# Attention value products reordered around two transposes, one MLP transpose moved, and stationary weight tiles shifted by 128 bytes

## The chip, the cores and the metric

The kernel runs on one core of a Trainium2 chip. The metric is device time in microseconds (us). The engines are named as in the profile: PE is TensorE (PEld its weight loads), ACT is ScalarE, DVE is VectorE, POOL is GpSimd, SP is SyncE, which issues most of the DMA transfers.

## The reference

One differential-attention layer and one MoBA block layer over 256 tokens of width 1024, each followed by a squared-ReLU MLP, all in float32:

```
def layer_step(h, layer):
    mix = diff_attention(h, ...) if layer == 0 else moba_attention(h, ...)
    h = layer_norm(ALPHA * h + mix, ln1_g[layer], ln1_b[layer])
    mlp = square(relu(h @ w_up[layer])) @ w_down[layer]
    return layer_norm(ALPHA * h + mlp, ln2_g[layer], ln2_b[layer])

# diff_attention, per head of 128 value columns (8 heads, two score maps each):
a = softmax(s1) - lam * softmax(s2)          # causal, with a relative-position bias
o = a @ v
o = o * rsqrt(mean(o * o) + eps) * subln_g * (1 - lam_init)
mix = o.reshape(256, 1024) @ w_out
```

The 256 tokens form two blocks of 128 queries, called halves here (h = 0 and 1).

## The kernel before

**Weights.** The weights arrive as 96 units of 128 x 2048, 48 for each layer, and each unit in two pieces of 1024 columns. SP fetches a piece into one of five `raw` tiles. `head()` has ACT round it to the high part `whi`; `piece()` has DVE form the low part `wlo` = raw - whi and then issues the fetch five pieces on. The parts live in seven `whi` and seven `wlo` tiles that are reused in turn. `bg(n)` puts up to n such pieces between other work; when it is not forced it goes by a credit that matmuls earn.

**Products.** Every operand of a product is split in high and low parts, and `three()` issues three matmuls for each product: high by high, and the two mixed ones. It has two forms. In the row form (lines 141 to 143) an activation block is the stationary operand and 512 (at the very end 256) columns of the weights stream past it. In the stationary form (lines 145 to 147) a 128 x 128 block of the weights is the stationary operand and 256 token columns of the activations stream past it. The trace names the moving operand first, then the stationary one: `whi,act_hi` at line 141, `act_hi,whi` at line 145. The stationary form makes a part of the projections ahead of both attentions and the MLP's up products of column groups 2 to 7; the row form makes the rest, among it the values, the output projection (`mix`), the up products of groups 0 and 1 (`up_rows`) and the down products.

**The end of the first attention.** Pairs 0 to 7 are the heads. For each, `turn(p)` transposes the softmaxed scores on PE (line 515) into a bank of the two `ps_c`, `turned(p)` has ACT copy that bank to `aT` (line 524), and `values(p)` multiplies by V (lines 539 to 541) into two of the four `ps_a` banks: one 128-column matmul for the first half of the queries and two for the second. The heads' output O is collected four heads at a time: `rms` squares it on ACT (line 575, eight squares), makes the reciprocal root on DVE or POOL, `scale(h)` multiplies a half (line 581). `o_turn(p0, h)` then transposes a half of four heads on PE (line 292, four matmuls into a `ps_c` bank), and ACT and DVE split it into `act_hi` (line 72) and `act_lo` (line 76), which `mix` uses as stationary operand. `mix(h, c, G0)` sums over heads 0 to 3, `mix(h, c, G1)` over heads 4 to 7.

**The MLP.** The column groups 0 and 1 are made in row form: `up_rows(c, h, g)` gives half h of group c, `g` is the half of the inner sum. `square` on ACT makes the squared ReLU, and `up_turn(c, h)` transposes it on PE (line 776, four matmuls). From group 2 on, `up(c, j)` uses the stationary form.

Engines run their instructions in program order, which is the order of the code; nothing else sorts them. The SBUF places follow from the tile pools. Every `whi` and `wlo` tile starts 192 bytes past a multiple of 256; the activations' tiles (`act_hi`, `act_lo`, `h_hi`, `h_lo`) start 128 bytes past one. These places were read from the built kernels, not from the trace.

Of the kernel before, what the change touches and what calls it, by code (L numbers as in the profile page):

```python
# [21 lines left out]
F32R = mybir.dt.float32r  # L22
# [30 lines left out]
def trunk(ctx: ExitStack, tc: tile.TileContext, x, first, units, lam_a, subln, rel_bias,  # L53
# [7 lines left out]
    dram = ctx.enter_context(tc.tile_pool(name="dram", bufs=1, space=bass.MemoryType.DRAM))  # L61


    small.tile([P, 24], F32, name="pad", bufs=1)

    def bank(tag):
        return psum.tile([P, 512], F32, name="ps_" + tag, tag=tag,
                         bufs={"a": 4, "b": 2, "c": 2}[tag])
# [16 lines left out]
    def fetch(q):  # L85

        if q < NU * PER:
            v, s = divmod(q, PER)
            raws[q] = wpool.tile([P, PIECE], F32, name="raw", bufs=RAWS)
            nc.sync.dma_start(raws[q], units[v, s])  # L90

    def head():

        v, s = divmod(state["head"], PER)
        if v >= NU:
            return False
        if s == 0 and v not in split:
            if v >= AHEAD and v - AHEAD not in free:
                return False
            split[v] = (wpool.tile([P, 2048], F32R, name="whi", bufs=AHEAD),  # L100
                        wpool.tile([P, 2048], F32R, name="wlo", bufs=AHEAD))
        c = slice(s * PIECE, (s + 1) * PIECE)
        nc.scalar.activation(split[v][0][:, c], raws[state["head"]], AF.Copy)  # L103
        state["head"] += 1
        return True
# [15 lines left out]
    def bg(most=8, force=False):  # L121

        while most > 0 and (force or state["credit"] >= 1.0 / PER):
            if not piece():
                state["credit"] = min(state["credit"], 1.0)
                return
            state["credit"] -= 1.0 / PER
            most -= 1
# [209 lines left out]
    def attention(layer, u0):  # L338
# [4 lines left out]
        with tc.tile_pool(name=f"attn{layer}", bufs=2) as pool, \  # L343
# [19 lines left out]
            def v_first(u):  # L363

                if u == 0:
                    for h in range(2):
                        pv[0, h] = bank("a")
                split[u] = (wpool.tile([P, 2048], F32R, name="whi", bufs=AHEAD),
                            wpool.tile([P, 2048], F32R, name="wlo", bufs=AHEAD))
                hi, lo = (w.rearrange("p (k c) -> p k c", k=4) for w in split[u])  # L370
                for k in range(4):
                    kk = 4 * u + k
                    split_to(act[0][:, kk], act[1][:, kk], chunks[kk][:, :S])
                    split_to(hi[:, k], lo[:, k], chunks[kk][:, S:])
                    if 2 <= kk < NK - 1:
                        fetch(kk + 2)
                    if kk == 6:
                        nc.scalar.dma_start(scr, line)
                    a = [at(kk, h) for h in range(2)]
                    for h in range(2):  # L380
                        nc.tensor.matmul(pv[0, h], a[h][0], hi[:, k], start=kk == 0, stop=False)  # L381
                    for h in range(2):
                        nc.tensor.matmul(pv[0, h], a[h][1], hi[:, k], start=False, stop=False)
                    for h in range(2):
                        nc.tensor.matmul(pv[0, h], a[h][0], lo[:, k], start=False, stop=kk == NK - 1)
                state["piece"] = state["head"] = (u + 1) * PER
                state["credit"] += PACE
                used.add(u)
# [139 lines left out]
                        nc.vector.tensor_copy(dst, src[:, :, ::-1])  # L528
                AT[p] = a

            def values(p):

                a = AT.pop(p)
                if diff:
                    if p % 4 == 0:
                        po[0], po[1] = bank("a"), bank("a")
                    c = slice(p * P, (p + 1) * P)
                    o = slice((p % 4) * P, (p % 4 + 1) * P)
                    nc.tensor.matmul(po[0][:, o], a[:, 0, 0:128], V[:, 0, c], start=True, stop=True)
                    nc.tensor.matmul(po[1][:, o], a[:, 0, 128:256], V[:, 0, c], start=True, stop=False)  # L540
                    nc.tensor.matmul(po[1][:, o], a[:, 0, 256:384], V[:, 1, c], start=False, stop=True)
                    return
                if p % 2 == 0:
                    po[p] = bank("a")
                o = po[p - p % 2][:, (p % 2) * S:(p % 2 + 1) * S]

                r = [slice(m * 64, (m + 1) * 64) for m in range(2)]
                v = [slice((2 * p + m) * 64, (2 * p + m + 1) * 64) for m in range(2)]
                for m in range(2):
                    nc.tensor.matmul(o[r[m]], V[:, 0, v[m]], a[:, m, 0:256], start=True, stop=False)  # L550
                for m in range(2):
                    nc.tensor.matmul(o[r[m], 128:], V[:, 1, v[m]], a[:, m, 256:384], start=False, stop=True)
# [33 lines left out]
            def o_turn(p0, h):  # L586
                transposed(O[p0][:, h], p0, h, gsub, True)
# [53 lines left out]
            if diff:  # L641
                turn(5)
                v_unit(u0 + 10, 1, 0)
                halves_hi(7)
                softmax_a(6)
                halves_lo(7)
                turned(5)
                scale = rms(0, [O[0][:, h] for h in range(2)], nc.gpsimd)
                bg(1)
                softmax_b(6)  # L650
                scores(7)
                turn(6)
                v_unit(u0 + 11, 1, 1)
                turned(6)
                softmax_a(7)
                bg(1, True)
                softmax_b(7)
                for h in range(2):
                    v_out(1, h)
                for h in range(2):  # L660
                    scale(h)
                bg(1, True)
                turn(7)
                turned(7)
                o_turn(0, 0)
                o_turn(0, 1)
                bg(2, True)
                for p in range(4, 8):
                    values(p)
                mix(0, 0, G0)  # L670
                scale = rms(4, po, nc.vector)
                scale(0)
                scale(1)
                bg(3, True)
                mix(0, 1, G0)
                mix(1, 0, G0[:2])
                o_turn(4, 0)
                mix(1, 0, G0[2:])
                o_turn(4, 1)
                bg(2, True)  # L680
                for c in range(2):
                    mix(0, c, G1)
                    if c == 0:
                        bg(1, True)
                    ln_add(0, c * 512, c * 512 + 512, pw[0, c])
                ln_apply(layer, 0, 512)
                bg(1, True)
                mix(1, 1, G0)
            else:
                turn(5)  # L690
                mix(0, 0, G0[:2])
                values(4)
                turned(5)
                mix(0, 0, G0[2:])
                halves_hi(7)
                softmax_a(6)
                halves_lo(7)
                softmax_b(6)
                scores(7)
                values(5)  # L700
                turn(6)
                mix(0, 1, G0)
                softmax_a(7)
                turned(6)
                collect(4)
                bg(1, True)
                softmax_b(7)
                bg(1, True)
                values(6)
                mix(1, 0, G0)  # L710
                turn(7)
                turned(7)
                bg(2, True)
                mix(0, 0, G1[:2])
                values(7)
                collect(6)
                mix(0, 1, G1[:2])
                bg(1, True)
                for c in range(2):
                    mix(0, c, G1[2:])  # L720
                    ln_add(0, c * 512, c * 512 + 512, pw[0, c])
                ln_apply(layer, 0, 512)
                mix(1, 1, G0)
# [16 lines left out]
    def mlp(layer, u0, then):  # L740
# [3 lines left out]
        with tc.tile_pool(name=f"mlp{layer}", bufs=2) as pool:  # L744
# [13 lines left out]
            def up_rows(c, h, g, then=None):  # L758
                if g == 0:
                    SQ[c, h] = bank("b")  # L760
                hi, lo = unit(u0 + 2 * c + g, k=4)
                for k in range(4):
                    three(SQ[c, h], (hi[:, k], lo[:, k]), at(4 * g + k, h), True, 1 / 8,
                          g == 0 and k == 0, g == 1 and k == 3)
                    if then and k % 2 == 0:
                        then(k // 2)
                if h == 1:
                    used.add(u0 + 2 * c + g)
# [67 lines left out]
            up_turn(1, 0)  # L836
            bg(2)
            up_rows(1, 1, 0)
            bg(2)
            up_rows(1, 1, 1)  # L840
            SQ[1, 1] = square(SQ[1, 1])
            up_turn(0, 1)
            bg(2)
            up(2, 0)
            bg()
# [135 lines left out]
```

## Time and profile before

| what | value |
|---|---|
| median of 3 runs | 592.87 us (592.8 to 593.11) |
| the profiled execution's own time | 593.63 us |
| its span | 591.6 us |
| PE busy | 580.2 us, 98% |
| PEld / DVE / ACT / POOL busy | 87% / 64% / 54% / 2% |
| granted TensorE clock | 0.995 of full speed (1.00 in the stretches looked at) |

The span runs from the first to the last recorded instruction; the execution's own time has 2.03 us more around it. A prediction made in the span's microseconds is carried over to the median by the difference of 0.76 us between this execution's own time and the median.

### The profile page before, as it was taken

To read this page: it belongs to the slowest core of one execution; us is meant where nothing else is said; L and a number is where in the kernel's file an instruction comes from. 1 tells how busy PE (TensorE), PEld (TensorE's weight loads), DVE (VectorE), ACT (ScalarE), POOL (GpSimd) and SP (SyncE) were. 2 spreads that over 40 slices of the span, in tenths; PEclk is the share of its full clock that TensorE was granted. 3 is DMA by queue.
4 is the path that set the end of the run, shared out by engine and by line. 5 is a ranking of instruction groups with operands and counts; after the bars stand their busy time and mean duration, and the time that the engine had idled before them with its cause. 6 is when DMAs were issued, how large, how long until landed. Compare 5 with 4: busy or idle time off the path is not lost.

```text
span 591.6 us, 9649 instructions
## 1 busy us (share of the span) xinstructions
PE 580.2 (98%) x3768; PEld 515.6 (87%) x3768; DVE 378.5 (64%) x692; ACT 318.3 (54%) x540; POOL 13.1 (2%) x45
## 2 busy tenths in 40 slices
PE   9999999999999999999999999999999999999993
PEld 7999978889899899898889999878899899899883
DVE  5798778976744644543978677697785544554236
ACT  6676787257654655552447555642785564554100
POOL 2000020000000000000000000000000000000000
PEclk9999999999999999999999999999999999999998
DMA  8996736447745836755259744151798556553002
GB/s 300 327 337 229 243 116 212 174 150 268 271 172 207 277 126 237 248 168 191 83 170 344 256 150 155 54 178 36 242 324 288 175 183 214 187 170 107 1 0 71
DMA packets 35548, 113.03 MB, mean 191 GB/s; under 512 B 3872, under 2 KB 8880, under 8 KB 35504
## 3 DMA queue, kind: packets, MB, share of 16 engines
q1 hardware_dynamic: 34144, 107.95, 53.8%
q0 software_dynamic: 1152, 4.19, 2.4%
q8 instruction: 29, 0.48, 0.3%
q10 hardware_dynamic: 208, 0.29, 0.1%
q14 instruction: 15, 0.12, 0.1%
HBM read 111.35 MB, written 1.07 MB: 190 GB/s over the span
## 4 chain that ended last, share of the span: by engine, by line
PE 97%; DMA 1%; DVE 1%; ACT 0%; SPq 0%; issue 0%; DVEq 0%
PE ps_a L143 13%; PE ps_a L142 13%; PE ps_b L145 13%; PE ps_a L141 13%; PE ps_b L147 12%; PE ps_b L146 12%; PE ps_b L141 4%; PE ps_b L143 4%; PE ps_b L142 4%; PE ps_a L462 2%; PE ps_c L515 1%; PE ps_c L292 1%; DMA raw<-in_first 1%; PE ps_a L550 1%; PE ps_c L776 1%; PE ps_a L381 1%
## 5 line engine op out<-in xcount | busy, mean ns | idle before, releaser
L115 DVE TENSOR_TENSOR wlo<-raw,whi 128x1024 fp32r<-128x1024 f32 x188 | 222.8, 1220 | 55.1 <-ACT whi L103 54.7
L103 ACT ACTIVATE whi<-raw 128x1024 fp32r<-128x1024 f32 x188 | 190.1, 1052 | 71.6 <-PE ps_a L143 52.5
L145 PE MATMUL ps_b<-act_hi,whi 128*128 128x256 f32 x640 | 179.8, 281 | 0.0
L146 PE MATMUL ps_b<-act_lo,whi 128*128 128x256 f32 x640 | 177.5, 277 | 0.0
L147 PE MATMUL ps_b<-act_hi,wlo 128*128 128x256 f32 x640 | 177.5, 277 | 0.0
L145 PEld LDWEIGHTS ps_b<-act_hi,whi 128*128 128x128 f32 x640 | 120.2, 188 | 1.5 <-issue 0.7
L146 PEld LDWEIGHTS ps_b<-act_lo,whi 128*128 128x128 f32 x640 | 120.7, 189 | 0.5
L147 PEld LDWEIGHTS ps_b<-act_hi,wlo 128*128 128x128 f32 x640 | 120.3, 188 | 0.0
L143 PE MATMUL ps_a<-whi,h_lo 128*128 128x512 f32 x248 | 97.7, 394 | 0.0
L142 PE MATMUL ps_a<-wlo,h_hi 128*128 128x512 f32 x248 | 97.2, 392 | 0.0
L141 PE MATMUL ps_a<-whi,h_hi 128*128 128x512 f32 x248 | 96.5, 389 | 0.0
L74 DVE TENSOR_TENSOR h_lo<-sqr,h_hi 128x512 fp32r<-128x512 f32 x24 | 16.6, 693 | 77.7 <-ACT h_hi L72 77.7
L142 PEld LDWEIGHTS ps_a<-wlo,h_hi 128*128 128x128 f32 x248 | 46.6, 188 | 10.3
L141 PEld LDWEIGHTS ps_a<-whi,h_hi 128*128 128x128 f32 x248 | 46.6, 188 | 9.9
L143 PEld LDWEIGHTS ps_a<-whi,h_lo 128*128 128x128 f32 x248 | 46.6, 188 | 9.3
L753 ACT ACTIVATE relu<-ps_b 128x512 f32<-128x512 f32 x32 | 19.1, 596 | 65.9 <-PE ps_b L147 55.0
L482 ACT ACTIVATE t<-t,mx 128x256 f32<-128x256 f32 x64 | 28.4, 445 | 31.5 <-DVE mx L479 31.5
L141 PE MATMUL ps_b<-whi,act_hi 128*128 128x512 f32 x96 | 39.1, 407 | 0.0
L143 PE MATMUL ps_b<-whi,act_lo 128*128 128x512 f32 x96 | 37.7, 393 | 0.0
L142 PE MATMUL ps_b<-wlo,act_hi 128*128 128x512 f32 x96 | 37.6, 391 | 0.0
L141 PE MATMUL ps_a<-whi,act_hi 128*128 128x512 f32 x80 | 32.3, 403 | 0.0
L142 PE MATMUL ps_a<-wlo,act_hi 128*128 128x512 f32 x80 | 31.5, 393 | 0.0
(140 smaller groups left out, 587.3 us busy)
## 6 DMA issues: line engine op xcount, KB each, us to landing
raw<-in_units SPq DMA_DIRECT2D x188, 512.0 KB, 4.6
bias<-scr SPq DMA_DIRECT2D x16, 256.0 KB, 5.3
lnp<-in_ln_g POOLq DMA_DIRECT2D x4, 512.0 KB, 4.5
lnp<-in_ln_b POOLq DMA_DIRECT2D x4, 512.0 KB, 5.4
raw<-in_first SPq DMA_DIRECT2D x5, 384.0 KB, 6.6
xres<-in_x SPq DMA_DIRECT2D x1, 1024.0 KB, 5.9
out<-xres SPq DMA_DIRECT2D x2, 256.0 KB, 2.1
out<-xres SPq DMA_DIRECT2D x4, 128.0 KB, 1.9
```

The source lines that it names most:

```text
L74: nc.vector.tensor_tensor(lo, src, hi.bitcast(F32), op=ALU.subtract)
L103: nc.scalar.activation(split[v][0][:, c], raws[state["head"]], AF.Copy)
L115: nc.vector.tensor_tensor(split[v][1][:, c], raws.pop(state["piece"]), split[v][0][:, c].bitcast(F32), op=ALU.subtract)
L141: nc.tensor.matmul(ps, a[0], w[0], start=start, stop=False)
L142: nc.tensor.matmul(ps, a[0], w[1], start=False, stop=False)
L143: nc.tensor.matmul(ps, a[1], w[0], start=False, stop=stop)
L145: nc.tensor.matmul(ps, w[0], a[0], start=start, stop=False)
L146: nc.tensor.matmul(ps, w[0], a[1], start=False, stop=False)
L147: nc.tensor.matmul(ps, w[1], a[0], start=False, stop=stop)
L462: nc.tensor.matmul(sc[m][:, c:c + n], a[r, q], b[r, :n], start=i == 0, stop=i == 2)
L482: nc.scalar.activation(t[:, m, s], t[:, m, s], AF.Exp, bias=mx[:, m, j:j + 1], accum_out=sm[:, m, j:j + 1])
L753: nc.scalar.activation(r, ps, AF.Relu)
```

## The change

Four edits, made in all places at once:

- `values` can do one half of the queries alone. The last four pairs' values now stand ahead of and between the two turns of O's scaled halves: first half of pairs 4, 5, 6, second half of 4 and 5, `o_turn(0, 0)`, second half of 6, `o_turn(0, 1)`, then pair 7.
- One forced piece of weights is taken from ahead of `turn(7)`, and one is added after the norm (`ln_apply`), so that each piece in between is made one place later.
- `whi` and `wlo` get a tile of their own for each of the seven places and part, 32 floats (128 bytes) longer than before. `whi` of a unit used in stationary form starts 128 bytes into its tile and its `wlo` at the start; for other units it is the other way round. With the places that the pool gives these tiles, all parts of the units of the stationary form lie 64 bytes past a multiple of 256, and all parts of the others at 192 bytes as before. The activations' places are unchanged in this sense.
- In the MLP of both layers `up_turn(0, 1)` moves from after `up_rows(1, 1, 1)` to before it.

```diff
--- before.py
+++ after.py
@@ -61,7 +61,9 @@
     dram = ctx.enter_context(tc.tile_pool(name="dram", bufs=1, space=bass.MemoryType.DRAM))
 
 
+
     small.tile([P, 24], F32, name="pad", bufs=1)
+    SHIFT = 32
 
     def bank(tag):
         return psum.tile([P, 512], F32, name="ps_" + tag, tag=tag,
@@ -89,6 +91,21 @@
             raws[q] = wpool.tile([P, PIECE], F32, name="raw", bufs=RAWS)
             nc.sync.dma_start(raws[q], units[v, s])
 
+    def stationary(v):
+
+        layer, n = divmod(v, UNITS)
+        if n < 16:
+            return (2 if layer == 0 else 4) <= n < (10 if layer == 0 else 12)
+        return 20 <= n < 44 and n % 4 < 2
+
+    def new_halves(v):
+        halves = []
+        for i, n in enumerate(("whi", "wlo")):
+            t = wpool.tile([P, 2048 + SHIFT], F32R, name=n, tag=f"{n}{v % AHEAD}", bufs=1)
+            c = SHIFT * ((i + stationary(v)) % 2)
+            halves.append(t[:, c:c + 2048])
+        return tuple(halves)
+
     def head():
 
         v, s = divmod(state["head"], PER)
@@ -97,8 +114,7 @@
         if s == 0 and v not in split:
             if v >= AHEAD and v - AHEAD not in free:
                 return False
-            split[v] = (wpool.tile([P, 2048], F32R, name="whi", bufs=AHEAD),
-                        wpool.tile([P, 2048], F32R, name="wlo", bufs=AHEAD))
+            split[v] = new_halves(v)
         c = slice(s * PIECE, (s + 1) * PIECE)
         nc.scalar.activation(split[v][0][:, c], raws[state["head"]], AF.Copy)
         state["head"] += 1
@@ -365,8 +381,7 @@
                 if u == 0:
                     for h in range(2):
                         pv[0, h] = bank("a")
-                split[u] = (wpool.tile([P, 2048], F32R, name="whi", bufs=AHEAD),
-                            wpool.tile([P, 2048], F32R, name="wlo", bufs=AHEAD))
+                split[u] = new_halves(u)
                 hi, lo = (w.rearrange("p (k c) -> p k c", k=4) for w in split[u])
                 for k in range(4):
                     kk = 4 * u + k
@@ -528,17 +543,20 @@
                         nc.vector.tensor_copy(dst, src[:, :, ::-1])
                 AT[p] = a
 
-            def values(p):
-
-                a = AT.pop(p)
+            def values(p, halves=(0, 1)):
+
+                a = AT[p] if halves == (0,) else AT.pop(p)
                 if diff:
-                    if p % 4 == 0:
-                        po[0], po[1] = bank("a"), bank("a")
                     c = slice(p * P, (p + 1) * P)
                     o = slice((p % 4) * P, (p % 4 + 1) * P)
-                    nc.tensor.matmul(po[0][:, o], a[:, 0, 0:128], V[:, 0, c], start=True, stop=True)
-                    nc.tensor.matmul(po[1][:, o], a[:, 0, 128:256], V[:, 0, c], start=True, stop=False)
-                    nc.tensor.matmul(po[1][:, o], a[:, 0, 256:384], V[:, 1, c], start=False, stop=True)
+                    for h in halves:
+                        if p % 4 == 0:
+                            po[h] = bank("a")
+                        if h == 0:
+                            nc.tensor.matmul(po[0][:, o], a[:, 0, 0:128], V[:, 0, c], start=True, stop=True)
+                        else:
+                            nc.tensor.matmul(po[1][:, o], a[:, 0, 128:256], V[:, 0, c], start=True, stop=False)
+                            nc.tensor.matmul(po[1][:, o], a[:, 0, 256:384], V[:, 1, c], start=False, stop=True)
                     return
                 if p % 2 == 0:
                     po[p] = bank("a")
@@ -659,14 +677,17 @@
                     v_out(1, h)
                 for h in range(2):
                     scale(h)
-                bg(1, True)
                 turn(7)
                 turned(7)
+                for p in (4, 5, 6):
+                    values(p, (0,))
+                for p in (4, 5):
+                    values(p, (1,))
                 o_turn(0, 0)
+                values(6, (1,))
                 o_turn(0, 1)
+                values(7)
                 bg(2, True)
-                for p in range(4, 8):
-                    values(p)
                 mix(0, 0, G0)
                 scale = rms(4, po, nc.vector)
                 scale(0)
@@ -684,7 +705,7 @@
                         bg(1, True)
                     ln_add(0, c * 512, c * 512 + 512, pw[0, c])
                 ln_apply(layer, 0, 512)
-                bg(1, True)
+                bg(2, True)
                 mix(1, 1, G0)
             else:
                 turn(5)
@@ -836,10 +857,10 @@
             up_turn(1, 0)
             bg(2)
             up_rows(1, 1, 0)
+            up_turn(0, 1)
             bg(2)
             up_rows(1, 1, 1)
             SQ[1, 1] = square(SQ[1, 1])
-            up_turn(0, 1)
             bg(2)
             up(2, 0)
             bg()

```

How the instructions move, for the places the prediction speaks of. Numbers behind a name tell tiles of one name apart.

PE at the end of the first attention, before: `t_1217` are the scores of pair 7, `aT_1030` and `aT_1121` the turned scores of pairs 4 and 5, `o_1044` is O of pairs 0 to 3.

```order
L515 MATMUL ps_c_1249<-ident_88,t_1217 128x128 x3
L292 MATMUL ps_c_1255<-ident_88,o_1044 128x128 x4
L292 MATMUL ps_c_1262<-ident_88,o_1044 128x128 x4
L539 MATMUL ps_a_1279<-V_124,aT_1030 128x128
L540 MATMUL ps_a_1280<-V_124,aT_1030 128x128
L541 MATMUL ps_a_1280<-V_124,aT_1030 128x128
L539 MATMUL ps_a_1279<-V_124,aT_1121 128x128
```

PE in the same place in the changed kernel, where lines 556, 558 and 559 are the values and 308 is O's turn:

```order
L530 MATMUL ps_c_1245<-ident_88,t_1217 128x128 x3
L556 MATMUL ps_a_1251<-V_124,aT_1030 128x128
L556 MATMUL ps_a_1251<-V_124,aT_1121 128x128
L556 MATMUL ps_a_1251<-V_124,aT_1215 128x128
L558 MATMUL ps_a_1255<-V_124,aT_1030 128x128
L559 MATMUL ps_a_1255<-V_124,aT_1030 128x128
L558 MATMUL ps_a_1255<-V_124,aT_1121 128x128
L559 MATMUL ps_a_1255<-V_124,aT_1121 128x128
L308 MATMUL ps_c_1260<-ident_88,o_1044 128x128 x4
L558 MATMUL ps_a_1255<-V_124,aT_1215 128x128
L559 MATMUL ps_a_1255<-V_124,aT_1215 128x128
L308 MATMUL ps_c_1269<-ident_88,o_1044 128x128 x4
```

Before, both turns of O followed pair 7's turn at once and all twelve value products came behind them; now seven value products stand ahead of the first turn, two between the turns, and three behind the second.

ACT in the same stretch, before: `V` are the two copies of the last value columns, `act_hi` the two splits of O's turned halves.

```order
L349 ACTIVATE V<-ps_a 128x512 x2
L103 ACTIVATE whi<-raw 128x1024
L524 ACTIVATE aT<-ps_c 128x384
L72 ACTIVATE act_hi<-ps_c,gsub 128x4x128 x2
L103 ACTIVATE whi<-raw 128x1024 x2
L575 ACTIVATE sq,ss<-ps_a 128x128 x8
```

ACT in the same stretch, after:

```order
L365 ACTIVATE V<-ps_a 128x512 x2
L539 ACTIVATE aT<-ps_c 128x384
L74 ACTIVATE act_hi<-ps_c,gsub 128x4x128 x2
L119 ACTIVATE whi<-raw 128x1024 x2
L593 ACTIVATE sq,ss<-ps_a 128x128 x8
L119 ACTIVATE whi<-raw 128x1024 x3
```

One `whi` is gone from between the copies of V and pair 7's `aT`; the rest keeps its order, and the two `whi` and the eight squares still stand behind both splits.

PE in the MLP of the first layer, before: the last row-form product of `up_rows(1, 1, 1)`, the moved turn, and the first stationary products of group 2.

```order
L142 MATMUL ps_b<-wlo,act_hi 128x512
L143 MATMUL ps_b<-whi,act_lo 128x512
L776 MATMUL ps_c<-ident,sqr 128x128 x4
L145 MATMUL ps_b<-act_hi,whi 128x256
L146 MATMUL ps_b<-act_lo,whi 128x256
L147 MATMUL ps_b<-act_hi,wlo 128x256
```

PE in the changed kernel where that turn stands now, with the row form on both sides of it:

```order
L157 MATMUL ps_b<-whi,act_hi 128x512
L158 MATMUL ps_b<-wlo,act_hi 128x512
L159 MATMUL ps_b<-whi,act_lo 128x512
L797 MATMUL ps_c<-ident,sqr 128x128 x4
L157 MATMUL ps_b<-whi,act_hi 128x512
L158 MATMUL ps_b<-wlo,act_hi 128x512
L159 MATMUL ps_b<-whi,act_lo 128x512
```

The turn no longer parts the row form from the stationary form; that run of 96 stationary matmuls now follows a row-form matmul directly.

## Rows read from the trace of the kernel before

**Rows 1.** The page: busy time by engine, and the chain that ended last, by engine.

```profile
PE 580.2 (98%) x3768; PEld 515.6 (87%) x3768; DVE 378.5 (64%) x692; ACT 318.3 (54%) x540; POOL 13.1 (2%) x45
...
PE 97%; DMA 1%; DVE 1%; ACT 0%; SPq 0%; issue 0%; DVEq 0%
```

**Rows 2.** TensorE's waits: line, tile, what it waited for; total, times, longest (us).

```profile
PE ps_c L292 <- ACT aT L524: 0.6, 1, 0.6
PE ps_c L292 <- ACT V L349: 0.5, 1, 0.5
```

**Rows 3.** Timeline, all three engines, 84 to 91 us: start, length, work (us).

```profile
84.38 1.29 ACT L349 ACTIVATE V<-ps_a 128x512 f32<-128x512 f32 x2 [1.03 <-PE ps_a L143]
84.87 0.49 PE L515 MATMUL ps_c<-ident,t 128*128 128x128 f32 x3
84.97 1.29 DVE L581 TENSOR_TENSOR o<-o,rs_y 128x512 f32<-128x512 f32 x2 [1.26 <-POOL rs_y L257]
85.56 1.05 ACT L103 ACTIVATE whi<-raw 128x1024 fp32r<-128x1024 f32 x1
85.81 0.63 PE L292 MATMUL ps_c<-ident,o 128*128 128x128 f32 x4 [0.45 <-ACT V L349]
86.51 0.48 ACT L524 ACTIVATE aT<-ps_c 128x384 f32<-128x384 f32 x1
87.05 0.66 PE L292 MATMUL ps_c<-ident,o 128*128 128x128 f32 x4 [0.61 <-ACT aT L524]
87.54 0.39 PE L539 MATMUL ps_a<-V,aT 128*128 128x128 f32 x2
87.74 0.69 ACT L72 ACTIVATE act_hi<-ps_c,gsub 128x512 fp32r<-128x512 f32 x1 [0.17 <-PE ps_c L292]
88.33 1.99 ACT L103 ACTIVATE whi<-raw 128x1024 fp32r<-128x1024 f32 x2
90.14 0.48 PE L141 MATMUL ps_b<-whi,act_hi 128*128 128x512 f32 x1
90.22 0.27 ACT L575 ACTIVATE sq<-ps_a 128x128 f32<-128x128 f32 x1
```

**Rows 4.** The same timeline, 92 to 100 us.

```profile
92.41 0.17 DVE L272 SCALAR_TENSOR_TENSOR rs_w<-ss,R 128x8 f32<-128x8 f32 x1 [0.93 <-ACT sq L575]
94.24 1.29 DVE L581 TENSOR_TENSOR o<-ps_a,rs_y 128x512 f32<-128x512 f32 x2
95.45 3.48 DVE L115 TENSOR_TENSOR wlo<-raw,whi 128x1024 fp32r<-128x1024 f32 x3
98.85 0.74 DVE L76 SCALAR_TENSOR_TENSOR act_lo<-ps_c,gsub,act_hi 128x512 fp32r<-128x512 f32 x1
99.85 0.40 PE L143 MATMUL ps_b<-whi,act_lo 128*128 128x512 f32 x1
```

**Rows 5.** TensorE's timeline: first and last matmul of two runs of 96.

```profile
138.41 0.36 PE L145 MATMUL ps_b<-act_hi,whi 128*128 128x256 f32 x1
...
149.69 0.28 PE L147 MATMUL ps_b<-act_hi,wlo 128*128 128x256 f32 x1
...
161.25 0.28 PE L145 MATMUL ps_b<-act_hi,whi 128*128 128x256 f32 x1
...
172.04 0.28 PE L147 MATMUL ps_b<-act_hi,wlo 128*128 128x256 f32 x1
```

**Rows 6.** Groups by form over the whole span: count, busy us, mean ns.

```profile
L146 PE MATMUL ps_b<-act_lo,whi 128*128 128x256 f32 x640 | 177.5, 277 | 0.0
```

**Rows 7.** The same groups, 138.7 to 149.6 us.

```profile
L146 PE MATMUL ps_b<-act_lo,whi 128*128 128x256 f32 x32 | 9.0, 281 | 0.0
```

**Rows 8.** The same groups, 162 to 172 us.

```profile
L146 PE MATMUL ps_b<-act_lo,whi 128*128 128x256 f32 x31 | 8.6, 276 | 0.0
```

**Rows 9.** The same groups, 317 to 327 us.

```profile
L146 PE MATMUL ps_b<-act_lo,whi 128*128 128x256 f32 x29 | 8.1, 281 | 0.0
```

**Rows 10.** Groups by form, whole span: 256 columns of weights as moving operand.

```profile
L142 PE MATMUL ps_b<-wlo,h_hi 128*128 128x256 f32 x16 | 4.4, 276 | 0.0
```


## What the change was predicted to do

> **What bounds the kernel now.** I read the page first: PE is busy for 580.2 of 591.6 us, and the chain that ended last is PE for 97% [rows 1]. So only two kinds of saving exist, a gap on PE or a cheaper matmul; work taken from another engine is worth nothing unless PE waits for it. I then read PE's waits. In the middle of the span there are two, 0.5 and 0.6 us, both ahead of line 292, O's turn, at the end of the first attention [rows 2]. The timeline there shows them ahead of 85.81 and 87.05 us [rows 3]. The releaser named for the first is the second copy of V; since O's scaling on DVE begins at 84.97, covers two halves in 1.29 us and is what the turn reads, I take that as its true cause. The second waits for pair 7's `aT` (86.51), which frees the `ps_c` bank and stands behind a `whi` of 1.05 us on ACT. Last I compared matmuls of one form in different stretches. The stationary form has two durations: 281 ns in 138.7 to 149.6 us and in 317 to 327 us [rows 7, 9], 276 ns in 162 to 172 us [rows 8], with nothing waited for in any of them. The cadence follows: from first to last start of 96 matmuls it is 149.69 - 138.41 = 11.28 us in the one run and 172.04 - 161.25 = 10.79 us in the other [rows 5], 0.49 us apart.
>
> **The values and the turns.** In the changed order nothing that PE reaches is late: pair 7's turn starts at 84.87 as before, three first-half values can follow it, since the second half of V, which the later ones need, is copied by 84.38 + 1.29 = 85.67; O's first scaled half and `aT` of pair 7 (no longer behind a `whi`, so about 86.2) are there before the turns that now come at 86.8 and 87.7. The twelve values cost 90.14 - 87.54 = 2.60 us [rows 3], the two turns 87.54 - 87.05 = 0.49 each, and pair 7's turn about 0.36, three quarters of such a turn. So `mix` starts at 84.87 + 0.36 + 2.60 + 0.98 = 88.8 to 88.9 in place of 90.14: a gain of 1.25 us there.
>
> It doesn't all stay. The second turn of O stood at 87.05 and now stands behind nine values, at 84.87 + 0.36 + 9 x 0.22 + 0.49 = 87.7 to 87.8. Behind it on ACT, in program order, are its `act_hi` (now 87.74), two `whi` (88.33, 1.99 us) and only then the first of the eight squares (90.22) [rows 3]. All of them move by 0.7. From the squares the chain goes on DVE: reciprocal root (92.41), scaling (94.24), three `wlo` of 3.48 us together (95.45), then `act_lo` of heads 4 to 7 at 98.85 to 99.59 [rows 4], where DVE has no idle time between its scaling and that split. PE first uses that `act_lo` at 99.85 [rows 4]: it has 0.26 us to spare today. With the producer 0.7 us later, at 100.3, and PE 1.25 us earlier, at 98.6, PE waits some 1.7 to 1.8 us. The gain of 1.25 turns into a loss of **0.5 to 0.6 us**. I take 0.6; bounds: 0.4, if the ACT work shrinks its gaps a little, and a gain of 1.25, if DVE's order leaves `act_lo` in time.
>
> **The pieces of weights.** The forced piece leaves ACT and DVE ahead of pair 7 and comes back behind the norm. Each piece between is made one place later. The half unit that loses its place is used first 18 row-form matmuls into `mix`; at no less than the 0.22 us of a value product that is 4 us behind its start, 92.8 in the new order. It is now the first of the two `wlo` that stand at 89 to 91.5, so it is hidden. I take the added piece behind the norm at nothing, because PE still has the second half's `mix` to run there; without that cover it costs DVE's time for one, 3.48 / 3 = 1.2 us [rows 4]. The fetches keep their order and number.
>
> **The shifted tiles and the MLP's turn.** These meet in one place, the stationary form's cadence. It holds 1,920 matmuls, 640 at each line; their mean at line 146 is 177.5 / 640 = 277.3 ns [rows 6], that is (277.3 - 276) / (281 - 276) = 27% of the way to the slow duration. In starts, of the 0.49 us between the two runs 0.08 is the entry (the first matmul is 0.36 against 0.28 us [rows 5]), and 0.41 / 95 = 4.3 ns a matmul is the cadence: 27% of 1,920 x 4.3 ns = 2.2 us are lost to it. Three runs of 96 make 3 x 0.41 = 1.2 of that, those at 138 and 317 us and that of the second layer's MLP which answers to the first; the rest lies in shorter stretches of the first projections and in the first matmuls of quick runs. As the means are rounded to whole ns, I take 2.0. The row form with 256 columns at the end is the nearest thing to what the shift makes: the same 256 columns, but the weights move, and act and weight tiles lie 64 bytes apart the other way round. All three lines hold 276 ns there, in all 48 matmuls [rows 10]. The shift gives the stationary form just this relation of stationary to moving place (the weights at 192, now at 64, beside the activations at 128). So I take it that the slow cadence goes: **-2.0 us**; bounds -2.2 and, since no row shows these places in this form, if the new places bring the slow cadence everywhere, 73% of 1,920 x 4.3 ns = +6.0 us. The row form keeps its places and gets nothing.
>
> The third turn's move costs no instruction: its source is squared on ACT well before PE reaches the new place, four transposes cost the same there. It changes how the run at 138.41 is entered: from a row-form matmul, as the quick run at 161.25 is, and not from a turn. If the places make no difference, this alone may make two runs quick, 0.4 each, a gain of 0.8; but the run at 317 is slow [rows 9] after row-form matmuls, so nothing is the other bound. If the places cure all, it adds nothing.
>
> Sum: +0.6 - 2.0 = **-1.4 us**, 593.63 to 592.2 us of the execution's own time; the median of the runs stands 0.76 lower than that execution, so **591.5 us**.
>
> **A rule that speaks against it.** The row shows two durations for one instruction [rows 7, 8]; that says something outside the instruction's size sets them. The Trainium skill ("TensorE: Matmul & The Clock Gate", "Step-by-step: what each phase is for") states that PE reads the streaming operand and the next weights through two independent ports, so that the load takes nothing from the running matmul. By that, places of the one against the other would not matter, the term of 2.0 falls, and the sum would be +0.6 less at most the 0.8 of the turn; the traces can't decide it, since they hold no run of the stationary form at other places.
>
> **The rivals.**
> (B) The places don't matter. For it: the slow and the quick runs stand at the same places (all `whi` and `wlo` start 192 bytes past a multiple of 256), so place alone does not make a run slow [rows 7, 8]. Against it: only the other relation shows no slow one [rows 10]. Then +0.6 and -0.8 to 0 from the turn: -0.2 to +0.6, median 592.7 to 593.5, about 593.0. Within 0.2% (1.19 us, about what a measurement of this kernel can tell from no change). Chance 27%.
> (C) The late `act_lo` doesn't stall PE, because the squares start on time after all. For it: DVE idles for 0.93 us ahead of the root at 92.41 [rows 4], so a part of the chain is not DVE's own work. Against it: that idle time is spent on the squares, and ACT runs from 87.74 through to them with no gap [rows 3]. Then -1.25 - 2.0 = -3.2, median 589.7. Chance 12%.
> (D) Slower: the shift tips more of the stationary form into the slow cadence. It is decided where the slow share passes (1.19 - 0.6 + 2.2) / 8.3 = 34%, 8.3 us being 1,920 x 4.3 ns, only a little over today's 27%; at 60% it is +0.6 + 33% x 8.3 = +3.3, 596.2; at 100% +6.7, 599.6. For it: the runs in today's places show that the state persists once entered, 96 matmuls long, without a cause in the trace. Against it: rows 10's form. Chance 13%.
> Other mishaps, as a fetch that comes late behind the moved piece: 3%.
>
> **The numbers.** The forecast, chance 45%, has its own range of 590.6 (the stall 0.8 us shorter) to 592.1 (1.4 of the 2.0 found). To leave no more than 2 in 10 out, the range takes in B, to 594.0, and reaches to C's 589.6. Faster by over 0.2% (below 591.68): the larger part of the forecast, 0.35, and C, 0.12: 0.47. Within it: B's 0.27 and the rest of the forecast, 0.09: 0.36. Slower: D, 0.13, the mishaps, 0.03, and the forecast's last 0.01: 0.17.
>
> **What would show it.** PE's two waits ahead of O's turn are gone; the first row-form matmul of the output projection starts at about 88.9; the squares start at 90.9; a new PE wait of 1.7 to 1.8 us for `act_lo` stands near 98.6 to 100.4, in the third matmul of `mix(0, 0, G1)`. If that wait is missing, C holds. Every stretch of the stationary form reads 276 ns at all three of its lines, and a run of 96 spans 10.8 us; lines with 281 ns in the runs after 138 and 317 would refute the term of the places, 281 throughout would be D. The forecast is wrong most easily in that term: it rests on one form that shares the relation of places, not on the stationary form itself.

## The result, and the profile after

The changed kernel is slower: 600.5 us median (600.43 to 600.63, 4 runs) against 592.99 us, ratio 1.0121 with a 95% interval of 1.0108 to 1.0133, some 7.5 us. The prediction of 591.5 us, 589.6 to 594.0, was wrong, and in its sign. The time lies 0.9 us above rival D at its far end, 599.6.

The page of the changed kernel (span; busy time by engine; the chain that ended last):

```profile
span 598.5 us, 9650 instructions
...
PE 586.6 (98%) x3768; PEld 521.9 (87%) x3768; DVE 378.5 (63%) x692; ACT 319.1 (53%) x540; POOL 15.5 (3%) x45
...
PE 96%; DVE 2%; ACT 1%; issue 0%; DVEq 0%
```

PE's busy time grew by 6.4 us with the same 3,768 matmuls [rows 1]; most of the loss is inside matmuls, not in gaps. Its waits after, in the middle of the span:

```profile
PE ps_b L159 <- DVE act_lo L78: 1.6, 1, 1.6
PE ps_c L202 <- DVE lnp L195: 1.2, 1, 1.2
```

Both waits ahead of O's turn [rows 2] are gone and a new one of 1.6 us stands at the first use of the late `act_lo`, as predicted. (The wait of 1.2 us for `lnp` is at the very start and was there before.) The timeline of the stretch, where everything is 1.3 us later than before: 0.3 us from the start of the kernel, the rest from slow stationary runs that already lie ahead of it:

```profile
86.19 0.49 PE L530 MATMUL ps_c<-ident,t 128*128 128x128 f32 x3
...
89.60 0.69 ACT L74 ACTIVATE act_hi<-ps_c,gsub 128x512 fp32r<-128x512 f32 x1 [0.20 <-PE ps_c L308]
...
89.99 0.47 PE L157 MATMUL ps_b<-whi,act_hi 128*128 128x512 f32 x1
...
92.09 0.27 ACT L593 ACTIVATE sq<-ps_a 128x128 f32<-128x128 f32 x1
...
97.32 3.49 DVE L131 TENSOR_TENSOR wlo<-raw,whi 128x1024 fp32r<-128x1024 f32 x3
...
100.72 1.41 DVE L78 SCALAR_TENSOR_TENSOR act_lo<-ps_c,gsub,act_hi 128x512 fp32r<-128x512 f32 x2
...
101.52 0.50 PE L159 MATMUL ps_b<-whi,act_lo 128*128 128x512 f32 x1 [1.65 <-DVE act_lo L78]
```

From pair 7's turn to the first product of `mix` it is 89.99 - 86.19 = 3.80 us, before 90.14 - 84.87 = 5.27 [rows 3]. From the turn to the first use of the late `act_lo` it is 15.33 us, before 14.98 [rows 3, 4]: 0.35 us are lost here where 1.5 had been gained on the way. DVE goes from the three `wlo` to `act_lo` with no gap, and PE waits for it.

The rest is the stationary form: summed from start to start, its 1,920 matmuls take 229.2 us here and 223.4 before, 5.8 of the 6.9 us by which the two spans differ. The groups by form over the whole span: the stationary form's second line and the 256-column row form at the end:

```profile
L162 PE MATMUL ps_b<-act_lo,whi 128*128 128x256 f32 x640 | 178.6, 279 | 0.0
L158 PE MATMUL ps_b<-wlo,h_hi 128*128 128x256 f32 x16 | 4.5, 280 | 0.0
```

and the first and the last matmul of the run that stood at 138.41 before (a run of 96 is 96 matmuls of the stationary form in succession):

```profile
140.08 0.28 PE L161 MATMUL ps_b<-act_hi,whi 128*128 128x256 f32 x1
...
151.26 0.28 PE L163 MATMUL ps_b<-act_hi,wlo 128*128 128x256 f32 x1
```

Line 162 went from 277 to 279 ns [rows 6], the narrow products, whose places the change left alone, from 276 to 280 [rows 10]. A mean of 279 looks like a little. The starts tell more: this run of 96 spans 11.18 us, and so do all 14 runs of 96 in the trace (11.18 to 11.19). Before, 11 of the 14 spanned 10.8 [rows 5] and were quick, and 3 were slow. A slow step is 117.8 ns in both kernels, though a slow matmul's recorded length is 281 ns before and 279 after; so the starts, not the lengths, are what to read.

### The profile page after: what moved, and what is told of

The parts are those of the page before. It is cut to its first block, busy times and chain, and to the rows that moved or that the text cites. A ratio compares the mean times of both kernels' runs of the same rounds, so it can differ in the third digit from the quotient of the medians.

```text
span 598.5 us, 9650 instructions
## 1 busy us (share of the span) xinstructions
PE 586.6 (98%) x3768; PEld 521.9 (87%) x3768; DVE 378.5 (63%) x692; ACT 319.1 (53%) x540; POOL 15.5 (3%) x45
## 4 chain that ended last, share of the span: by engine, by line
PE 96%; DVE 2%; ACT 1%; issue 0%; DVEq 0%
PE ps_b L161 13%; PE ps_b L163 13%; PE ps_a L157 13%; PE ps_b L162 13%; PE ps_a L159 12%; PE ps_a L158 12%; PE ps_b L159 4%; PE ps_b L157 4%; PE ps_b L158 4%; PE ps_a L477 2%; PE ps_c L530 1%; PE ps_c L308 1%; PE ps_a L568 1%; PE ps_a L396 1%; PE ps_a L398 1%; PE ps_c L202 1%
## 5 line engine op out<-in xcount | busy, mean ns | idle before, releaser
L162 PEld LDWEIGHTS ps_b<-act_lo,whi 128*128 128x128 f32 x640 | 119.9, 187 | 0.6
L157 PE MATMUL ps_a<-whi,h_hi 128*128 128x512 f32 x248 | 97.9, 395 | 0.0
L159 PE MATMUL ps_a<-whi,act_lo 128*128 128x512 f32 x80 | 31.4, 392 | 0.0
```

Of the source, the lines that this page charges most:

```text
L157: nc.tensor.matmul(ps, a[0], w[0], start=start, stop=False)
L159: nc.tensor.matmul(ps, a[1], w[0], start=False, stop=stop)
L162: nc.tensor.matmul(ps, w[0], a[1], start=False, stop=False)
```

## The experiments

Each list of edits is against the kernel before, unless it says otherwise. Each time stands beside that of the kernel before on the same chip, which lies between 593.4 and 593.8 us there.

**The tiles alone (shift_only).** Only `new_halves` and its two uses, of which one is shown:

```diff
-            split[v] = (wpool.tile([P, 2048], F32R, name="whi", bufs=AHEAD), ...)
+            split[v] = new_halves(v)
```

> The kernel before with the new weight tiles alone (places and SHIFT as in the change; values, turns and MLP order as before). Theory 1 (the stationary form's cadence is set by the place of its weights, 64 past a multiple of 256): nearly all of its matmuls at about 280 ns and 117.8 ns apart, a run of 96 in 11.2 us, and +5.5 to +6.5 us, 598.5 to 599.5. Theory 2 (the attention edit is what disturbs the cadence): 592.9, within 0.5.

599.61 us against 593.81, ratio 1.0102 (1.0087 to 1.0117). By form:

```profile
L161 PE MATMUL ps_b<-act_lo,whi 128*128 128x256 f32 x640 | 178.7, 279 | 0.0
L157 PE MATMUL ps_b<-wlo,h_hi 128*128 128x256 f32 x16 | 4.5, 280 | 0.0
```

The tiles are most of the loss, 5.8 of the 7.5 us, with the cadence of the changed kernel and the narrow products slow too. Theory 1 holds against theory 2.

**The same tiles with every part at the old place (even_places).** Against shift_only:

```diff
-            c = SHIFT * ((i + stationary(v)) % 2)
+            c = SHIFT * i
```

> The kernel before with the longer tiles in the new arrangement (whi and wlo alternating), but every weight part 192 past a multiple of 256, as before. Theory 1a (the place within 256 bytes decides): the mix of quick and slow runs of before, 592.9 within 1. Theory 1b (the arrangement, that is the distance of whi from wlo and the tiles' other address bits, decides): slow cadence throughout, the 256-column products with moving weights at the end at 280 ns too, 598.5 to 599.5.

593.67 us against 593.81, ratio 0.9998 (0.9989 to 1.0007).

```profile
L161 PE MATMUL ps_b<-act_lo,whi 128*128 128x256 f32 x640 | 177.6, 278 | 0.0
L157 PE MATMUL ps_b<-wlo,h_hi 128*128 128x256 f32 x16 | 4.4, 276 | 0.0
```

The arrangement costs nothing; the 128 bytes do (1a, not 1b). The narrow products are at 276 ns again, though these two kernels hold their operands at the same places. What differs is what the stationary form did before them.

**The change without the tiles (no_shift).** The changed kernel with the tiles of before.

> The changed kernel with the weight tiles of before: the attention edit, the moved piece and the MLP's turn without the shift. Theory 1: the 7.5 us go but for the new wait for act_lo, so +0.5 (593.4), or -0.3 if the turn's move makes its two MLP runs quick. Theory 2: about 600.

593.42 us against 593.81, ratio 0.9998 (0.9989 to 1.0007). Its largest wait:

```profile
PE ps_b L144 <- DVE act_lo L77: 1.7, 1, 1.7
```

The wait for `act_lo` is there without the shifted tiles; the attention edit does not disturb the cadence.

**The MLP's turn alone (mlp_turn).**

```diff
             up_rows(1, 1, 0)
+            up_turn(0, 1)
             bg(2)
             up_rows(1, 1, 1)
             SQ[1, 1] = square(SQ[1, 1])
-            up_turn(0, 1)
             bg(2)
```

> The kernel before with up_turn(0, 1) moved alone, in both layers. If the entry from a turn is what makes the runs at 138 and 428 us slow: both at 276 ns, 10.8 us in place of 11.3 each, -0.8 to -1.0 us, 592.0. If not: 592.9 within 0.2, both runs still at 281 ns.

592.98 us against 593.81, ratio 0.9985 (0.9975 to 0.9995): a gain of some 0.9 us. The run in question:

```profile
139.03 0.28 PE L145 MATMUL ps_b<-act_hi,whi 128*128 128x256 f32 x1
...
149.81 0.28 PE L147 MATMUL ps_b<-act_hi,wlo 128*128 128x256 f32 x1
```

10.78 us in place of 11.28 [rows 5]; the same in the second layer. So these two runs, entered from the row form, become quick at the places of before. The row form ahead is not enough by itself: the run at 316 us also follows it and stays slow, and in this trace the first run (17.06 us) is slow, which was quick before (16.56), with nothing edited ahead of it. no_shift has this gain in it and is 0.44 us above mlp_turn, which is what the attention edit costs; the two intervals overlap, so the size is the trace's (0.35) as much as the times'.

**The activations moved instead of the weights (act_128, both_128, act_64, act_192).** `act_hi` and `act_lo` in tiles 256 bytes longer, 64, 128 or 192 bytes in; both_128 has the shifted weight tiles too:

```diff
+    ACT_SHIFT = 32        # 16 and 48 in the others
+    act = tuple(const.tile([P, NK * S + 64], F32R, name=n)[:, ACT_SHIFT:ACT_SHIFT + NK * S]
+                .rearrange("p (k s) -> p k s", k=NK) for n in ("act_hi", "act_lo"))
```

> The kernel before with act_hi and act_lo 128 bytes further in tiles 256 bytes longer, the weights where they were (192). The activations that stream in the stationary form now lie at 0, the weights 64 below that (192), the same difference within 256 bytes as in the changed kernel, but from the other side. Theory R (the difference of the two operands' places counts): slow cadence nearly throughout, 280 ns, +5 to +6.5 us. Theory W (the place of the weights alone counts): 276 ns in most runs as before, time within 1 us of before.

> The shifted weight tiles alone (as shift_only) and act_hi and act_lo 128 bytes further too: weights of the stationary form at 64, activations at 0, the difference of before again. Theory R: the slow cadence goes, within 1 us of before. Theory W: slow as shift_only, +5 to +6.5 us.

> The kernel before with act_hi and act_lo 64 bytes further, so that both operands of the stationary form lie at 192. Theory R says that the difference counts but not what none of it does: quick throughout (590.8) or slow throughout (599). Theory W: as before within 1 us.

> The kernel before with act_hi and act_lo 192 bytes further (at 64), half of 256 bytes away from the weights at 192. Theory R: another cadence than before, quick throughout (590.8) or slow throughout (599). Theory W: as before within 1 us.

One run each beside 593.53: 601.0, 599.09, 602.88 and 604.97 us. The second line of the stationary form in act_128, both_128, act_64 and act_192:

```profile
L146 PE MATMUL ps_b<-act_lo,whi 128*128 128x256 f32 x640 | 178.5, 279 | 0.0
```

```profile
L161 PE MATMUL ps_b<-act_lo,whi 128*128 128x256 f32 x640 | 178.5, 279 | 0.0
```

```profile
L146 PE MATMUL ps_b<-act_lo,whi 128*128 128x256 f32 x640 | 181.0, 283 | 0.0
```

```profile
L146 PE MATMUL ps_b<-act_lo,whi 128*128 128x256 f32 x640 | 180.8, 283 | 0.0
```

From the starts of matmuls (a step is the time from one start to the next), all at a granted clock of 1.00; the last column sums the steps of a form over the whole trace, less those of before:

| weights, activations (bytes past a multiple of 256) | steps, ns | runs of 96 | stationary form; row form, us |
|---|---|---|---|
| 192, 128 (before) | 113.3 or 117.8 | 11 quick, 3 slow | 0; 0 |
| 64, 128 (after, shift_only) | 117.8, few shorter runs 113.3 | 14 slow | +5.5; -0.3 (shift_only) |
| 192, 0 (act_128) | 117.8, few runs 113.3 | 1 quick, 13 slow | +5.4; +1.9 |
| 64, 0 (both_128) | 113.3 or 117.8 | 5 quick, 9 slow | +2.5; +2.8 |
| 192, 192 (act_64) | 120.0 | 14 at 11.4 to 11.5 us | +10.0; -0.8 |
| 192, 64 (act_192) | 118.7 to 120.0 | 14 at 11.3 to 11.5 us | +9.3; +1.9 |

Theory W falls: the weights never moved in act_128 and its stationary form is as slow as that of shift_only. Theory R holds in part. With the weights 64 above the activations, counted within 256 (first and fourth row), the quick step is found in many runs; with them 64 below (second and third) in nearly none; with 0 or 128 between them the steps are longer still. But both_128, with the difference of before, did not get the time of before: 9 runs are slow in place of 3, so the difference alone doesn't fix the cadence. Its time is no clean test either, since more than half of its loss lies in the row form, whose `act` operands moved too. And there the row form itself shows two steps: three matmuls of the down products, with both operands where they lay before, take 686.7 ns in some stretches and 700 in others.

**The row form with both operands at one place (move_same).** act_64 had shown one thing more: its row form was quicker. Here the units of the row form lie at 128, like their activations, those of the stationary form at 192 as before:

```diff
+            t = wpool.tile([P, 2048 + (48, 16)[i]], F32R, name=n, tag=f"{n}{v % AHEAD}", bufs=1)
+            c = (0 if stationary(v) else 48, 16 if stationary(v) else 0)[i]
```

> The kernel before with weight tiles in which the units of the row form lie at 128, where their stationary activations lie, and those of the stationary form at 192 as before. In act_64 the row form with both operands at one place took 226.7 ns a matmul against 229 to 230. If that holds for all of the row form: 1,234 matmuls by 2.6 ns, -3.2 us, if the stationary runs keep their mix of cadences; the entry from this row form may turn them slow, up to +6. Rival: the row form's gain in act_64 was of the activations' place and not of the two being equal: no change within 1 us.

595.57 us against 593.76, ratio 1.0033 (1.002 to 1.0046). The first and last of 48 row-form matmuls between two stationary runs, in move_same, and then before:

```profile
172.24 0.40 PE L155 MATMUL ps_a<-whi,h_hi 128*128 128x512 f32 x1
...
182.92 0.39 PE L157 MATMUL ps_a<-whi,h_lo 128*128 128x512 f32 x1
```

```profile
172.15 0.39 PE L141 MATMUL ps_a<-whi,h_hi 128*128 128x512 f32 x1
...
182.91 0.39 PE L143 MATMUL ps_a<-whi,h_lo 128*128 128x512 f32 x1
```

10.68 against 10.76 us, with slower first steps in the former; in the middle three matmuls take 680 ns and before 686.7. That gain is real, 1.7 us over the kernel when the steps of the row form are summed, about half of the 3.2 expected. But the runs of 96 that follow the row form are all slow now, with their places unchanged, and those that follow a turn (`sqr`) are quick: the reverse of before. So what a run is entered from bears on which of the two steps it keeps.

The entry can be read from the starts. In the ten traces with the stationary form's operands at 192 and 128 (before, even_places, no_shift, mlp_turn, move_same and the five below), 130 runs of 96 follow a row-form matmul. The step from that matmul to the run's first is 225 to 228 ns wherever the run then steps 117.8 ns (35 of them), and 230 to 237 ns wherever it comes to 113.3 (95). At other places this doesn't hold: shift_only enters at 230 to 233 ns and steps 117.8 in each. What sets the entry step is not shown.

**All together (best, best_same).** The attention edit with its pieces spread (attn_fix, below) and the MLP's turn, with the tiles of before and with those of move_same.

> attn_fix and the MLP's turn moved, weight tiles as before. If the two add up: 1.2 and 0.9 us, 2.1 us below before (ratio 0.9965).

> best with the weight tiles of move_same. If all three add up: 2.1 + 3.2 = 5.3 us below before (ratio 0.991); if the stationary runs turn slow after the new row form, up to 6 us of it are lost.

best: 592.68 us against 593.76, ratio 0.9986 (0.9976 to 0.9995). best_same: 596.58, ratio 1.005 (1.0035 to 1.0065). The sums of the expectations both failed, best because of attn_fix; best_same, 2.8 us above before, lies beyond even its worse branch (5.3 gained, up to 6 lost). In best_same the turn's move works the other way: the run behind `up_rows(1, 1, 1)`, by form in 140 to 148 us, in move_same (entered from a turn) and best_same (from the row form):

```profile
L160 PE MATMUL ps_b<-act_lo,whi 128*128 128x256 f32 x25 | 6.9, 277 | 0.0
```

```profile
L161 PE MATMUL ps_b<-act_lo,whi 128*128 128x256 f32 x24 | 6.8, 282 | 0.0
```

**The pieces of weights spread (attn_fix).** The attention edit with tiles and MLP as before; the lines are against that edit:

```diff
-                bg(3, True)
+                bg(1, True)
                 mix(0, 1, G0)
                 mix(1, 0, G0[:2])
                 o_turn(4, 0)
+                bg(1, True)
                 mix(1, 0, G0[2:])
                 o_turn(4, 1)
-                bg(2, True)
+                bg(3, True)
```

> The kernel before with the attention edit, and the three weight pieces that stood ahead of act_lo of heads 4 to 7 spread: one ahead, one between O's two turns, one behind. If the three pieces on DVE are what made act_lo late: PE's wait of 1.7 us is gone and the edit gives its 1.2 us, 592.4 beside 593.6 of before on that chip. If the whole DVE chain is late: a wait of over 0.5 us stays and the gain is under 0.6.

593.54 us against 593.76, ratio 0.9999 (0.9989 to 1.0009). The wait that the prediction named is gone, and so is the gain; a wait of 0.7 us is there as the second theory has it, but at another place, the next norm. PE's waits, and DVE there:

```profile
PE ps_b L144 <- DVE act_lo L75: 0.7, 1, 0.7
PE ps_c L293 <- issue: 0.3, 1, 0.3
```

```profile
99.85 4.62 DVE L116 TENSOR_TENSOR wlo<-raw,whi 128x1024 fp32r<-128x1024 f32 x4
...
104.39 0.69 DVE L311 SCALAR_TENSOR_TENSOR xres<-xres,ps_b 128x512 f32<-128x512 f32 x1
...
109.46 0.75 DVE L331 SCALAR_TENSOR_TENSOR xres<-xres,rs_y,lnp 128x512 f32<-128x512 f32 x1
...
111.58 2.35 DVE L116 TENSOR_TENSOR wlo<-raw,whi 128x1024 fp32r<-128x1024 f32 x2
...
113.85 0.68 DVE L75 TENSOR_TENSOR act_lo<-ps_c,act_hi 128x512 fp32r<-128x512 f32 x1
```

DVE has no gap from 95.7 to 115 us. The turn of the normed rows (line 293, at 110.31) comes 0.1 us behind the norm's end at 109.46 + 0.75, so I read its 0.3 us, put down to "issue", as a wait for DVE; the 0.7 us are for the norm's own `act_lo` (line 75), behind the two `wlo` at 111.58, one of which is the piece that the change puts behind `ln_apply`.

**A piece made where DVE stood idle (attn_idle, best_idle).** Against attn_fix (and best):

```diff
                 turned(7)
+                bg(1, True)
...
                 o_turn(4, 1)
-                bg(3, True)
+                bg(2, True)
```

> attn_fix gave no gain: its trace shows DVE busy without a gap from 95.7 to 115 us and PE waiting 0.3 and 0.7 us at the next norm instead. Here one more weight piece is made behind pair 7's turn, where DVE stood idle before act_lo of the first heads, and one fewer in the stretch that DVE fills. If DVE's work in that stretch is what took the gain: no wait of PE over 0.3 us between 86 and 116 us and 1.0 to 1.2 us below before. If something else sets the norm's time: the waits stay, within 0.4 us of before.

> attn_idle and the MLP's turn moved, weight tiles as before: if DVE was the cause and the edits add up, 1.9 to 2.1 us below before, ratio 0.9965; if not, 0.8 below as best, ratio 0.9986.

attn_idle: 592.39 us against 593.44, ratio 0.9983 (0.9974 to 0.9992). best_idle: 591.55 us, ratio 0.9964 (0.9952 to 0.9976), below both kernels of this study. PE's waits in attn_idle, all there are, and DVE:

```profile
PE ps_c L187 <- DVE lnp L180: 1.2, 1, 1.2
```

```profile
86.33 1.22 DVE L116 TENSOR_TENSOR wlo<-raw,whi 128x1024 fp32r<-128x1024 f32 x1
...
99.72 3.48 DVE L116 TENSOR_TENSOR wlo<-raw,whi 128x1024 fp32r<-128x1024 f32 x3
...
103.13 0.68 DVE L311 SCALAR_TENSOR_TENSOR xres<-xres,ps_b 128x512 f32<-128x512 f32 x1
...
112.57 0.68 DVE L75 TENSOR_TENSOR act_lo<-ps_c,act_hi 128x512 fp32r<-128x512 f32 x1
```

The extra piece runs at 86.33, where DVE stood idle for 2.14 us in attn_fix; everything behind comes 1.3 us earlier, `act_lo` at 112.57 in place of 113.85, and no wait is left. So DVE's load was the cause, and it adds to the turn's gain.

## Why the prediction was wrong, point by point

**The values and the turns: right in mechanism and sign.** The two waits went, the `mix` began 3.80 us after pair 7's turn (predicted about 3.9), the squares stand 2.1 us behind the `mix` as expected (92.09; 90.9 against 88.9 was 2.0), and the wait for `act_lo` measured 1.6 to 1.7 us (predicted 1.7 to 1.8). Net 0.35 to 0.44 lost, predicted 0.6. Rival C was wrong. The prediction put the first of the two old waits down to O's scaling and not to V, as the row had it; the trace of mlp_turn names that scaling (`o`) for the same 0.5 us.

**The pieces of weights: mis-sized where their cover was named.** The piece behind the norm was priced at nothing, covered by the second half's `mix`, with 1.2 us as its price if the cover fails. In the changed kernel no wait shows it, and I read that as PE being 1.6 us late by then: the norm's `act_lo` starts at 114.03 in no_shift and at 113.85 in attn_fix, and PE waits for it only in attn_fix. There, with the earlier wait removed, this piece and DVE's load ahead of it took the gain back.

**The shifted tiles: the step that failed.** It was "The shift gives the stationary form just this relation of stationary to moving place ... So I take it that the slow cadence goes: -2.0 us". It measured +5.8 us (shift_only), the bound of +6.0 that the same step had given as its other end. Three things were wrong with it. The nearest row was the narrow row form at 276 ns [rows 10], taken as a property of its places; in shift_only and the changed kernel the same products, at the same places, step 117.8 ns. Either step can hold there, depending on what ran before, so a quick row is no evidence on places. The runs at 138 and 161 us, one slow and one quick at the same places [rows 7, 8], already said that places alone don't set it: the text counted that for rival B and not against its own term. And the term was too large by its own measure: it took recorded lengths for the share of the slow cadence, 27%, where by the starts 384 of the 1,920 matmuls, 20%, stand where the step is 117.8 ns throughout, worth some 1.6 us.

The Trainium skill ("TensorE: Matmul & The Clock Gate", "Step-by-step: what each phase is for") states that loading the next tile's weights takes no read bandwidth of the SBUF from the running matmul. By that rule the shift would have cost nothing. The runs disagree with that conclusion for this kernel: 128 bytes, all else equal, cost 5.9 us (shift_only against even_places). That the two reads disturb each other is a guess that no run here shows.

**The MLP's turn: right as a bound, lost in the sum.** Moved alone it gives 0.8 to 0.9 us, the far end of "two runs quick, 0.4 each" (0.50 each, since the dearer entry goes too). With the shifted tiles no run is quick, and only that entry is left, 0.08 us a run (11.27 in shift_only, 11.19 in the changed kernel).

**The chances.** D's mechanism, the slow step spreading over the stationary form, is what happened, to the full, and it had 13%. Its price was near, +6.7 us (599.6) against +7.5. The edits moved one by one don't add up to 7.5: shift_only is +5.8 and the attention edit 0.35 to 0.44; the 1.3 us left, which the intervals of the two times nearly cover, are not traced to an edit.

What stays open is why a place makes a step, and what it is in the entry that picks one: no run here shows what PE does inside a matmul.

## What to carry to other kernels

Where one matmul form shows two durations in one trace with nothing waited for, list every run of it by first and last start, with what was ahead of it and the step into it, before any edit that moves its operands; a form that shares some property of it is no substitute. A move of operands by a fraction of 256 bytes is a change in itself and deserves a run by itself, apart from edits of the order. And when a wait is removed from an engine that is 98% busy, follow the engine that fed it to the next place where it is due: here DVE was full for 19 us, and only work put into its idle time turned the edit into a gain.

## What the runs showed of the hardware

- The step of the stationary form (256 columns) is one of a few fixed values that most runs keep for all their 96 matmuls, or from the sixth on: 113.3, 117.8 or, with both operands at one place, 120.0 ns. In move_same, where the narrow products (256 columns of weights moving) have both operands at one place, they step 119.9.
- The row form (512 columns) is quicker with both operands at one place, 680 against 686.7 ns for three matmuls (move_same, before); the stationary form has its longest step there (120.0, act_64).
- At the same places either step can hold, and what ran before bears on it across many matmuls: the narrow products at the end step 117.8 ns in shift_only and 113.3 in even_places, in both behind 120 other row-form matmuls. The step isn't simply handed on: in act_64 they step 113.3 ns, though its stationary runs step 120.0.
- At 192 and 128 bytes, the step into a run of 96 from the row form tells its cadence in ten traces: 225 to 228 ns ahead of the 35 that step 117.8, 230 to 237 ahead of the 95 that come to 113.3.
